# A 128-byte store per partition on the queue of ScalarE, ahead of the bulk stores of a half-rotary kernel

## Chip, cores, metric

One NeuronCore of a Trainium2 chip. The metric is the device time of one execution in microseconds (us), the median of several. The profile's span, from the first to the last instruction, is some 2 us shorter. The medians of the kernel before on different occasions, on chips that the record numbers 1, 2 and 4, differ by up to 0.5 us, so each kernel is compared with runs of the kernel before in the same rounds.

## The reference

```python
batch, seq, heads, dim = (16, 512, 16, 64)          # x: float32; cos, sin: (512, 32)
x1, x2 = x[..., :32], x[..., 32:]
first  = x1[..., :16] * cos[..., :16] - x1[..., 16:] * sin[..., :16]
second = x1[..., :16] * sin[..., :16] + x1[..., 16:] * cos[..., :16]
return np.concatenate([first, second, x2], axis=-1)
```

Half of each head is rotated; the other half, x2, is copied. In a loaded tile x2 is therefore final at once. 33.6 MB come in and 33.6 MB go out.

## The kernel before

The input is cut into four tiles of 8.4 MB, each 128 partitions of 16 sequence rows (64 KB of a partition). Three tiles are held in SBUF at a time. VectorE rotates in place, and each tile is stored from where it was loaded. All bulk transfers go through the queue of SyncE.

```python
ring = const_pool.tile([P, NS, K, H, D], fp32)      # NS = 3 slots, K = 16 rows, H = 16, D = 64
def rows(t, lo, hi):
    return ring[:, t % NS, lo:hi].rearrange("p k h d -> p (k h d)")
def load(t, lo=0, hi=K):
    nc.sync.dma_start(out=rows(t, lo, hi), in_=xf[t, :, lo * R : hi * R])
def store(t, lo=0, hi=K):
    nc.sync.dma_start(out=of[t, :, lo * R : hi * R], in_=rows(t, lo, hi))
# ... zeroed tile, loads of cos and sin on the GpSimd queue ...
load(0, 0, K0)          # K0 = 4:  16 KB per partition
load(0, K0, K)          #          48 KB
load(1)                 #          64 KB
load(2, 0, KC)          # KC = 8:  32 KB
# ... VectorE spreads cos and sin over the partitions ...
rotate(0, 0, K0); rotate(0, K0, 10); rotate(0, 10, K)    # four VectorE instructions each
store(0)
load(2, KC, K)
load(3)                 # same slot as tile 0: waits for store(0)
for t in range(1, T):
    rotate(t, 0, KC); rotate(t, KC, K)
    store(t)
```

A scheduler orders the instructions and puts a semaphore wait wherever two of them touch the same bytes, in SBUF or in the output.

## Time and profile before

| | before |
|---|---|
| device time, median of 4 runs | 162.95 us (162.76 to 162.98) |
| span of the profiled run | 160.9 us |
| VectorE busy | 70% of the span |
| packets of the SyncE queue, share of 16 DMA engines | 97.7% |
| ScalarE | no work |

The profile has three views that matter here. The table of DMA queues says how full the 16 DMA engines are. The chain that ended last says which waits the end hangs on. The timeline says when each transfer was issued. Under these lies the trace's record of every DMA packet: start, duration, size, queue. Put in order, those records make 16 strings, one per engine, in which each packet starts when the one before ends. "Excess" is the duration of a packet above the duration that its size usually has, as a mean over the 16 engines. A "row" is the part of a transfer that lies in one partition; in the records it is one packet. A "turn" is the place in a string where rows of a load are followed by rows of a store, or the reverse; where two queues have work, "one row per turn" means one small row after each packet of the other queue. A transfer has "landed" when its semaphore reports all of it as done. The prediction shows the lines of the page that carry the argument.

### The profile page before, as it was taken

What the parts mean: (1) busy time and instruction counts of PE and PEld (TensorE: products, weight loads), DVE (VectorE), ACT (ScalarE), POOL (GpSimd) and SP (SyncE); (2) the same over time, 40 slices, a digit from 0 to 9 for tenths busy, and PEclk for the clock granted to TensorE, in tenths of its full rate; (3) what the DMA queues carried; (4) which work ended last, traced back from release to release, by engine and by line L of the source; (5) the groups of instructions that cost most, each with busy time, mean ns of one, the idle gap of its engine ahead of it and who ended that gap; (6) DMA issues with size and microseconds to landing.
All of it is one profiled execution on the core that took longest, in us unless ns stands there. A gap on an engine that the chain in (4) does not pass through costs nothing.

```text
span 160.9 us, 116 instructions
## 1 busy us (share of the span) xinstructions
DVE 112.9 (70%) x47; POOL 1.4 (1%) x6
## 2 busy tenths in 40 slices
DVE  1049999999999999999999991699999900000000
POOL 3000000000000000000000000000000000000000
DMA  6999999969999996999996996998998998998992
GB/s 195 554 391 391 391 456 521 521 261 521 391 391 261 521 521 261 521 391 391 472 570 261 521 521 261 521 423 358 521 423 358 521 423 358 521 423 358 521 423 98
DMA packets 1504, 67.24 MB, mean 418 GB/s; under 512 B 192, under 2 KB 192, under 8 KB 224
## 3 DMA queue, kind: packets, MB, share of 16 engines
q1 hardware_dynamic: 1440, 67.11, 97.7%
q0 software_dynamic: 64, 0.13, 0.2%
HBM read 33.69 MB, written 33.55 MB: 418 GB/s over the span
## 4 chain that ended last, share of the span: by engine, by line
DMA 50%; DVE 28%; DVEq 1%; issue 0%; SPq 0%
DMA ring<-in_x_dram 31%; DMA out_dram<-ring 18%; DVE b_t L98 10%; DVE ring L99 10%; DVE ring L100 5%; DVE ring L103 3%; DVEq L142 1%; SPq L55 0%; DVEq L98 0%
## 5 line engine op out<-in xcount | busy, mean ns | idle before, releaser
L98 DVE TENSOR_TENSOR b_t<-ring,table 128x4096 f32<-128x4096 f32 (+2 forms) x9 | 35.6, 3959 | 5.4 <-DMA ring<-in_x_dram 5.2
L99 DVE TENSOR_TENSOR ring<-ring,table 128x4096 f32<-128x4096 f32 (+2 forms) x9 | 35.6, 3950 | 0.3
L100 DVE TENSOR_TENSOR ring<-ring,b_t 128x2048 f32<-128x2048 f32 (+2 forms) x9 | 18.4, 2049 | 0.3
L103 DVE TENSOR_TENSOR ring<-ring,b_t 128x2048 f32<-128x2048 f32 (+2 forms) x9 | 18.4, 2042 | 0.0
L74 DVE LOAD_MASK_SELECT spun<-stage x1 | 0.0, 14 | 8.7 <-DMA stage<-in_sin_dram 8.7
L84 DVE COPY table<-packed 32x1024 f32<-32x1024 f32 x4 | 2.7, 684 | 0.1
L81 DVE COPY packed<-spun 32x512 f32<-32x512 f32 (+3 forms) x4 | 1.7, 416 | 0.1
L61 DVE MEMSET stage<- 128x512 f32 x1 | 0.5, 485 | 0.9 <-PEq L131 0.9
L74 DVE STREAM_SHUFFLE spun<-stage 128x512 f32<-128x512 f32 x1 | 0.7, 722 | 0.0
L63 POOL DMA_DIRECT2D stage<-in_cos_dram x1 | 0.6, 649 | 1.3 <-DVE stage L61 1.3
L64 POOL DMA_DIRECT2D stage<-in_sin_dram x1 | 0.5, 532 | 0.0
L131 POOL MEMSET const-bfloat16-1.0<- 128x1 bf16 x1 | 0.1, 96 | 0.0
L131 POOL MEMSET const-float32-0.0<- 128x1 f32 x1 | 0.1, 93 | 0.2 <-issue 0.2
L131 POOL MEMSET const-float32-1.0<- 128x1 f32 x1 | 0.1, 93 | 0.0
L131 POOL MEMSET const-uint8-127<- 128x1 uint8 x1 | 0.1, 93 | 0.0
## 6 DMA issues: line engine op xcount, KB each, us to landing
ring<-in_x_dram SPq DMA_DIRECT2D x2, 4096.0 KB, 44.9
ring<-in_x_dram SPq DMA_DIRECT2D x1, 6144.0 KB, 21.6
ring<-in_x_dram SPq DMA_DIRECT2D x1, 2048.0 KB, 7.7
stage<-in_cos_dram POOLq DMA_DIRECT2D x1, 64.0 KB, 6.3
stage<-in_sin_dram POOLq DMA_DIRECT2D x1, 64.0 KB, 7.7
out_dram<-ring SPq DMA_DIRECT2D x4, 37.2
ring<-in_x_dram SPq DMA_DIRECT2D x2, 34.7
```

Source lines behind the costliest of these rows:

```text
L61: nc.vector.memset(stage[:, :, :, 0:Q], 0.0)
L63: nc.gpsimd.dma_start(out=spread[:, 0, 0], in_=cosf)
L64: nc.gpsimd.dma_start(out=spread[:, 0, 1], in_=sinf)
L74: nc.vector.stream_shuffle(out=spun[:], in_=stage.rearrange("p t k j -> p (t k) j")[:, :, 0:Q], mask=[j % PQ * REP for j in range(PB)],)
L81: nc.vector.tensor_copy(out=packed[0:n], in_=spun[q * PB : q * PB + n])
L84: nc.vector.tensor_copy(out=table[r * PB : (r + 1) * PB].rearrange("p t k c j -> p (t k) c j"), in_=packed.unsqueeze(2).to_broadcast((PB, ...
L98: nc.vector.tensor_mul(out=b_t, in0=x1, in1=s)
L99: nc.vector.tensor_mul(out=x1, in0=x1, in1=c)
L100: nc.vector.tensor_sub(out=x1[:, :, :, 0:Q], in0=x1[:, :, :, 0:Q], in1=b_t[:, :, :, Q:HF])
L103: nc.vector.tensor_add(out=x1[:, :, :, Q:HF], in0=x1[:, :, :, Q:HF], in1=b_t[:, :, :, 0:Q])
L131: nc = _bacc.Bacc("TRN2", target_bir_lowering=False, num_devices=1)
L142: with _tile.TileContext(nc) as tc:
```

## The change

128 bytes of each partition (columns 32 to 63 of head 0, row 0 of tile 0), already final, go to the output on the queue of ScalarE as soon as the first load has landed. Store 0 writes them again later. The evident intent is to have some writing done, or begun, early on a queue that is otherwise unused.

```diff
     load(0, 0, K0)
+
+    nc.scalar.dma_start(out=of[0, :, HF:D], in_=ring[:, 0, 0, 0, HF:D])
     load(0, K0, K)
     load(1)
     load(2, 0, KC)
```

## The prediction

> **What bounds the kernel now.** I read the page from the top: busy shares first, then the DMA queues, then the chain that ended last, then the timeline of the first 45 us, and last the trace's own record of every DMA packet.
>
> The page, its busy shares, its 40 slices and its DMA queues:
>
> ```profile
> DVE 112.9 (70%) x47; POOL 1.4 (1%) x6
> ...
> DMA  6999999969999996999996996998998998998992
> ...
> DMA packets 1504, 67.24 MB, mean 418 GB/s; under 512 B 192, under 2 KB 192, under 8 KB 224
> ...
> q1 hardware_dynamic: 1440, 67.11, 97.7%
> q0 software_dynamic: 64, 0.13, 0.2%
> ```
>
> VectorE, the only computing engine, works for 70% of the span. The packets of the hardware queue fill 97.7% of all 16 DMA engines' time. The row of digits has no hole after the first slice. 1440 packets are ten transfers of 128 rows plus 16 completion packets each: one packet per partition row, whatever its length, eight rows and one completion per engine and transfer. No ScalarE row exists: that engine does nothing now.
>
> The chain that ended last, in order of time (start, length, what), shows the same from the other side:
>
> ```profile
> 1.17 21.62 DMA ring<-in_x_dram
> ...
> 29.68 1.75 DVE ring L100
> 31.44 1.68 DVE ring L103
> 33.12 0.02 issue
> 33.14 3.38 DVE b_t L98
> ...
> 43.37 29.64 DMA out_dram<-ring
> 73.02 0.02 issue
> 73.03 28.86 DMA ring<-in_x_dram
> ```
>
> The chain runs through VectorE in places, but its DMA pieces are 29 us long for transfers of 8.4 MB, which alone need some 19.3 us: they stand in a queue. So the VectorE pieces are not what sets the end; the queue is full throughout, and the kernel ends when 67.1 MB have passed. The timeline of the start:
>
> ```profile
> 0.74 1.89 SPq L55 DMA_DIRECT2D ring<-in_x_dram  x4
> ...
> 17.87 2.29 DVE L99 TENSOR_TENSOR ring<-ring,table 128x2048 f32<-128x2048 f32 x1
> 20.20 1.22 DVE L100 TENSOR_TENSOR ring<-ring,b_t 128x1024 f32<-128x1024 f32 x1
> 21.34 1.21 DVE L103 TENSOR_TENSOR ring<-ring,b_t 128x1024 f32<-128x1024 f32 x1
> 22.89 3.37 DVE L98 TENSOR_TENSOR b_t<-ring,table 128x3072 f32<-128x3072 f32 x1 [0.34 <-DMA ring<-in_x_dram]
> ...
> 43.37 0.35 SPq L58 DMA_DIRECT2D out_dram<-ring  x1
> ```
>
> Four loads (21.0 MB) are queued by 2.6 us; the first store joins at 43.4 us, about ten before the queue would run dry (the fourth load lands at 53.3 us).
>
> **The packet records.** Ordered by start and put end to end they make 16 strings without holes (0.05 us of idle each, on the mean). A packet has a set duration by size: 159 ns for 4 KB, 608 for 16 KB, 1213 for 32 KB, 1815 for 48 KB, 2418 for 64 KB; a straight line with 12 ns of fixed cost and 36.7 ns per KB, which is 434 GB/s over 16 engines. A string lasts from about 1.9 us to 159.2 us, 157.3 us, and its packets at set durations make 155.4. The difference, 2.3 us by packet durations, lies in three places and almost nowhere else: the first packets (0.65 us, start-up); the last two rows of the load that precedes the first store (0.90 us and 0.47 us above the set duration, mean of 16 engines, starting at 48.7 us); and the last row of the load that precedes the second store (0.25 us). There are only two load-to-store turns, and store-to-load turns show no excess. So the first turn costs 1.37 us and the second 0.25 us. The 1.12 us between them is the price of being the first store, and the one thing that an early small store could buy back.
>
> **What the Trainium skill says.** "DMA: Bandwidth & Descriptors", section "Issuing engines are not separate DMA queues": transfers begun by ScalarE, SyncE or GpSimd run on the same 16 DMA engines and interleave. The trace agrees: the 64 GpSimd packets sit inside the same 16 strings. Section "Queues, rings and completion order" of that page: each engine goes round the queues that have work, a packet at a time. It agrees again: the table loads' 4 KB packets alternate one to one with the 16 KB packets of the load. Section "Specifications" there: under 512 B the engine does read-modify-write. The 128 B rows here are under it; no transfer of data in the present trace is, so its price is open. "Perfetto Trace Analysis", section "What "DMA-bound" means": large descriptors matter where the engines bind. The 12 ns of fixed cost against 2418 ns for 64 KB says this kernel already has them.
>
> **The change part by part.** Nothing is removed; store 0 writes the same bytes again later.
>
> 1. Added on ScalarE: one wait for the first load and one DMA issue. The load lands 7.7 us after 0.74 us, 8.4 us. ScalarE is empty; an issue takes about 0.4 us on SyncE, which issues nothing more at that time. Cost on the path: none.
>
> 2. Added on the DMA engines: 128 rows of 128 B, 16 KB, plus 16 completions; eight rows and one completion per engine. By the straight line (an estimate, below the smallest data packet seen) a row is 12 + 4.6, about 17 ns; a completion is 9 ns in the records: 8 x 17 + 9 = 0.145 us per engine. The engines bind, so all of it is on the path: +0.15 us.
>
> 3. Landing. The first packet of the first load began 1.0 us after its issue, so these packets stand ready at about 9.6 to 10 us. At one small packet per 48 KB packet, nine turns of about 1.83 us bring the landing to about 26 or 27 us; if one turn takes several rows, to about 14 us.
>
> 4. New waits. VectorE writes columns 0 to 31 of each head, the new store reads columns 32 to 63. I expect no wait: in the chain every dependent VectorE pair has an "issue" of 0.02 us between, and L100 and L103, which write interleaved quarters of the same rows, have none, and overlap by 0.08 us. So the tracking sees interleaved columns as separate. Store 0 (same output bytes) and the load of tile 3 into the same slot must wait for the new store; at 43.4 us and 73.0 us both come well after 27 us. Cost: none.
>
> 5. Moved: the first write to the output and the first read of SBUF by these engines, from 48.7 us to about 10 us, on another queue. If the 1.12 us is a price paid once per engine, and a small packet of another queue can pay it while the loads go on, the later turn drops to about 0.25 us: -1.12 us.
>
> Sum if bought back: 162.96 + 0.15 - 1.12 = 161.99 us.
>
> **The rivals.** (a) Price moved, not saved: the excess sits on load packets that were in flight, so whatever stalled there held up other data too, and would do so at 10 us as well; the engines bind at both times. Time: 162.96 + 0.15 = 163.1 us. For it: nothing in the strings ever overlaps. Against it: the stalled packets belonged to the same queue as the store, and another queue may not block it. (b) Small writes cost more than their line: each of eight rows is its own load-to-store turn or a read-modify-write. At 0.25 us a turn, 8 x 0.25 = 2.0 us at most, 162.96 + 2.0 + 0.15 less up to 1.12: 164.0 to 165.1 us. For it: the second turn shows that a turn isn't free. Against it: that turn preceded 64 KB rows, 512 times as long. (c) VectorE waits after all: L99 would start at about 27 instead of 17.9 us, and store 0 be issued at about 52.5 us, with 1.0 us to its first packet: the queue, dry at about 53.2 us, would stand empty some 0.3 us, and over a microsecond if the landing is a turn late. Later stores have slack of several us. Time: 163.3 to 164.5 us. Against it stands the overlap of L100 and L103.
>
> **Range and chances.** I give 0.5 to bought back in whole or part (162.0 to 162.6), 0.35 to moved (163.1), 0.15 to (b) or (c) (163.3 and up). The middle of that is about 162.4 us. The kernel's own spread is 0.2 us. A range of 161.6 to 163.8 us should hold it 8 times in 10. Two per cent is 3.3 us: faster than 159.7 would need more than the whole 2.3 us of excess, so 0.01; slower than 166.2 needs (b) at its full size and more, so 0.02; within 0.97.
>
> **What would show it.** A third queue with 144 packets and 336 instead of 192 packets under 512 B; the first 48 KB and 64 KB packets at their set durations (against a and b); the last two rows before store 0 about 0.12 us instead of 0.69 us above theirs on the mean; VectorE's L99 still at 17.9 us (against c). The prediction is wrong if the 128 B packets take far more than 17 ns, if excess appears on the load packets beside them, or if the 1.37 us stays where it is, which would say that the turn's cost goes with this queue, or these row sizes, and not with being first.

## The result

The changed kernel took 163.16 us (median of 4 runs, 163.06 to 163.28) against 162.95 us. The ratio of the fast runs is 1.0016, 95% interval 0.9999 to 1.0033: the same, if anything 0.2 us slower. The time lies in the predicted range, 0.8 us above the predicted 162.4, and next to the 163.1 of rival (a).

The page of the changed kernel, its DMA queues and the issue that was added (size, then us from issue to landing):

```profile
DMA packets 1648, 67.26 MB, mean 418 GB/s; under 512 B 336, under 2 KB 336, under 8 KB 368
...
q1 hardware_dynamic: 1440, 67.11, 97.5%
q0 software_dynamic: 64, 0.13, 0.2%
q10 hardware_dynamic: 144, 0.02, 0.1%
...
out_dram<-ring ACTq DMA_DIRECT2D x1, 16.0 KB, 19.2
```

The third queue is there with its 144 packets: 128 rows and 16 completions. It takes 0.1% of the engines' time, but its 16 KB need 19.2 us to land. The timeline of the changed kernel:

```profile
8.54 0.37 ACTq L67 DMA_DIRECT2D out_dram<-ring  x1
...
17.67 2.29 DVE L101 TENSOR_TENSOR ring<-ring,table 128x2048 f32<-128x2048 f32 x1
19.99 1.22 DVE L102 TENSOR_TENSOR ring<-ring,b_t 128x1024 f32<-128x1024 f32 x1
21.13 1.21 DVE L105 TENSOR_TENSOR ring<-ring,b_t 128x1024 f32<-128x1024 f32 x1
...
43.43 0.35 SPq L58 DMA_DIRECT2D out_dram<-ring  x1
```

L101 is the former L99, the first VectorE write into the tile that the new store reads. It starts at 17.67 us, ten microseconds before that store lands, so it doesn't wait. Store 0 is issued at 43.43 us, as before (43.37). Store 0 does have the new wait; the waits of SyncE's own queue show it:

```profile
SPq L58 <- DMA out_dram<-ring: 4.8, 1, 4.8
```

SyncE stands at it from 22.9 to 27.7 us, and would have waited for VectorE until 43.4 us anyway. The later pieces of the chain that ended last have the length that they had:

```profile
43.43 29.62 DMA out_dram<-ring
...
73.07 28.91 DMA ring<-in_x_dram
```

What was to shrink did not. The rows around the turn from loads to store 0, from the packet records of both kernels (mean start and end in us, bytes, excess in us):

```
before   47.66 -> 48.87   32768 B   0.002
         48.87 -> 50.99   32768 B   0.903    last two rows of the load
         51.02 -> 52.70   32768 B   0.468
         52.70 -> 55.12   65536 B   0.000    first row of store 0

after    47.66 -> 48.87   32768 B   0.000
         48.87 -> 50.80   32768 B   0.717
         50.81 -> 52.63   32768 B   0.603
         52.63 -> 55.05   65536 B   0.000
```

1.37 us before, 1.32 us after, in the same place. Nor is there any excess where the new rows run: every 48 KB row keeps 1.815 us, every 128 B row is recorded with 13 ns.

### The profile page after: what moved, and what is told of

Its sections match the earlier page's. It is cut to its first block, busy times and chain, and to the rows that moved or that the text cites. A ratio compares the mean times of both kernels' runs of the same rounds, so it can differ in the third digit from the quotient of the medians.

```text
span 161.0 us, 118 instructions
## 1 busy us (share of the span) xinstructions
DVE 112.9 (70%) x47; POOL 1.4 (1%) x6
## 4 chain that ended last, share of the span: by engine, by line
DMA 50%; DVE 28%; DVEq 1%; issue 0%; SPq 0%
DMA ring<-in_x_dram 31%; DMA out_dram<-ring 18%; DVE b_t L100 10%; DVE ring L101 10%; DVE ring L102 5%; DVE ring L105 3%; DVEq L144 1%; SPq L55 0%; DVEq L100 0%
## 5 line engine op out<-in xcount | busy, mean ns | idle before, releaser
L101 DVE TENSOR_TENSOR ring<-ring,table 128x4096 f32<-128x4096 f32 (+2 forms) x9 | 35.6, 3950 | 0.3
## 6 DMA issues: line engine op xcount, KB each, us to landing
out_dram<-ring ACTq DMA_DIRECT2D x1, 16.0 KB, 19.2
```

The lines of the kernel that those rows point to most:

```text
L101: nc.vector.tensor_mul(out=x1, in0=x1, in1=c)
```

## The experiments

Two theories stood at the start. R: the excess belongs to the 32 KB rows that happen to precede store 0, and has nothing to do with being first. F: it belongs to the first store of the SyncE queue, so a store on another queue can't pay it.

**E1, the changed kernel again**, to size its loss.

> The changed kernel as it is, on the chip and in the rounds of the next three, to size its small loss and to see whether its packet pattern repeats. Theory A (the added packets are pure queue time: 8 rows of 13 ns and one completion of 9 ns per engine): +0.11 us, ratio about 1.0007. Theory B (the third queue also costs something at the start or the end): +0.2 us or more, ratio 1.0013 or above. In the packets: the last two 32 KB rows before store 0 are again about 0.7 and 0.6 us above 1.213 us.

162.68 us against 162.59 us, ratio 1.0006 (0.9994 to 1.0019). That agrees with the 0.11 us of queue time of theory A. The excess before store 0 is there again, 1.15 us, though spread as 0.43 and 0.72 us and not as 0.7 and 0.6. Whether the 0.2 us of the first comparison has another part is below what these runs resolve.

**E2, other rows before store 0.**

```diff
-    load(1)
     load(2, 0, KC)
+    load(1)
```

> The kernel before, without the early store, with the loads of tile 1 and of the first half of tile 2 swapped, so that the rows just before store 0 are 64 KB and not 32 KB. Theory R (the 1.37 us of the first load-to-store turn belong to the 32 KB rows): the excess at that turn falls to about 0.25 us, as at the second turn, and the time to about 161.9 us, ratio 0.993. Theory F (it belongs to being the first store of the SyncE queue): the excess stays at about 1.4 us and the time at 163.0 us, ratio 1.000. In both VectorE gets tile 1 later, by some 10 us, and has the slack for it.

162.71 us, ratio 1.0000 (0.9987 to 1.0013). With 64 KB rows the excess is 1.36 us, all on the last row. R has fallen. The timeline of this kernel also clears VectorE:

```profile
43.40 0.35 SPq L58 DMA_DIRECT2D out_dram<-ring  x1
43.79 0.43 SPq L55 DMA_DIRECT2D ring<-in_x_dram  x1
53.31 4.43 DVE L98 TENSOR_TENSOR b_t<-ring,table 128x4096 f32<-128x4096 f32 x1 [9.93 <-DMA ring<-in_x_dram]
```

VectorE is idle for 9.93 us, through the whole turn (48.8 to 52.6 us), so its SBUF traffic isn't what slows those rows.

**E3, 32 KB rows before the second turn.**

```diff
-    load(3)
+    load(3, 0, KC)
+    load(3, KC, K)
```

> The kernel before with the load of tile 3 cut into two halves of 32 KB rows, so that the second load-to-store turn has 32 KB rows as the first has. Theory R (row size): the excess at the second turn rises from 0.25 to about 1.4 us, and the time by about 1.1 us to 164.1 us, ratio 1.007. Theory F (first store of the queue): the second turn stays at about 0.25 us and the time at 163.0 us, ratio 1.000. VectorE can start on half of tile 3 earlier in both; it has slack anyway.

162.53 us, ratio 0.9996 (0.9981 to 1.0010). The second turn has 0.02 us of excess, the first 1.36 us. R falls from this side too.

**E4, the early store on the queue of SyncE itself**, from a zeroed tile, overwritten later by store 0.

```diff
+    nc.vector.memset(zero, 0.0)          # a new 128 x 32 tile
...
     load(0, K0, K)
+    nc.sync.dma_start(out=of[0, :, HF:D], in_=zero)
     load(1)
```

> The kernel before with a 128-byte store per partition (zeros, overwritten later by store 0, so the result is right) on the queue of SyncE itself, behind the two loads of tile 0. Theory F (the price is paid once per queue and engine by its first store): the excess shows on the rows before this small store, at about 22 us, or not at all, and the turn before store 0 falls to about 0.25 us; time between 162.0 us (if the small store hides it) and 163.1 us (if it only moves it). Theory R (row size): the turn before store 0 stays at about 1.4 us and the time is 163.0 to 163.1 us.

162.90 us, ratio 1.0020 (1.0008 to 1.0032). No excess before the small store at 22 us, and 1.14 us before store 0 as ever. F, as stated, has fallen: a first store of the same queue doesn't pay if it is this small. In the records an engine's eight small rows begin some 9 ns apart: from the end of its last 48 KB row to the start of its first 64 KB row there are 84 ns, against 2 ns in the kernel before. So the rows account for 0.08 us of the 0.3 us by which this kernel is longer; the rest is not explained.

**A new theory, F2:** the excess is paid by the first *bulk* store, wherever it stands. Its rivals: G, every turn to a store that has loads behind it costs this much; T, it is tied to store 0 or to its place in time.

**E6, an early bulk store** of zeros, 16 KB per partition, on the queue of SyncE; it adds 2.1 MB.

```diff
     load(0, K0, K)
+    nc.vector.memset(rows(2, KC, KC + K0), 0.0)
+    nc.sync.dma_start(out=of[0, :, 0 : K0 * R], in_=rows(2, KC, KC + K0))
     load(1)
```

> The kernel before with an early bulk store on the queue of SyncE, behind the two loads of tile 0: 16 KB of zeros from each partition, 2.1 MB, into output rows that store 0 overwrites later (the result is right). It adds 8 packets of 0.61 us per engine, 4.9 us of queue time. Theory F2 (the excess is paid by the first bulk store, wherever it stands): an excess of about 1.3 us shows on the last rows before this early store, at about 20 us, and the turn before store 0 falls to 0 to 0.4 us; time about 162.7 + 4.9 = 167.6 us. Theory G (every turn to a large store that is followed by loads costs 1.3 us): both turns show about 1.3 us; time about 168.9 us. Theory T (it is tied to store 0 or to its place in time): nothing at the early store, 1.3 us at store 0; 167.6 us.

167.95 us, ratio 1.0313 (1.0290 to 1.0335), 5.1 us more by the ratio for 4.9 us of added rows. The packet records (columns as above):

```
 18.59 -> 20.42   49152 B   0.017
 20.43 -> 23.52   49152 B   1.276    last row of the load before the early store
 23.52 -> 24.13   16384 B   0.000    first row of the early store
...
 54.96 -> 56.18   32768 B   0.000
 56.17 -> 57.68   32768 B   0.296    last row of the load before store 0
 57.68 -> 60.10   65536 B   0.000    first row of store 0
```

The price has moved to the early store, and store 0 is down to what a second turn costs. G and T fall. But it has *moved*: the total excess is 2.34 us, in the kernel before 2.33.

**E7, a first turn ten microseconds later**, with tile 2 loaded whole before store 0; the trace shows that the scheduler then also put store 1 ahead of load 3.

```diff
-    load(2, 0, KC)
+    load(2)
...
-    load(2, KC, K)
```

> The kernel before with tile 2 loaded whole before store 0, so that the first store comes about 10 us later and is followed by store 1, not by a load. It will be slower for a hole in the queue later; only the turn is looked at. Theory F2 (first bulk store): about 1.3 us of excess on the rows that end at about 62 us. Theory G (a store that is followed by loads): 0 to 0.4 us there. Theory T (place in time): nothing at the turn, some excess at about 49 us.

```profile
43.39 27.23 SPq L58 DMA_DIRECT2D out_dram<-ring  x2
...
82.09 0.34 SPq L55 DMA_DIRECT2D ring<-in_x_dram  x1
```

One run, 171.78 us, its state unknown; only the turn counts. 1.31 us of excess on the last 64 KB row, 58.46 to 62.18 us, nothing at 49 us. The price follows the first bulk store and not the clock, as F2 says.

**E10, how large is bulk?** E6 with 4 KB rows, 0.5 MB.

```diff
+    nc.vector.memset(rows(2, KC, KC + 1), 0.0)
+    nc.sync.dma_start(out=of[0, :, 0:R], in_=rows(2, KC, KC + 1))
```

> The early store of zeros on the queue of SyncE with 4 KB rows in place of 16 KB, 0.5 MB, 1.3 us of queue time: between the 128 B that paid nothing and the 16 KB that paid 1.28 us. If the excess goes with the bytes of store that stand behind loads in flight, a part of it (0.2 to 0.9 us) shows before this store at about 20 us and the rest before store 0; if it is all or nothing above some size, 1.3 us shows at one of the two places and 0 to 0.4 us at the other. Time about 162.7 + 1.3 = 164.0 us in either case.

One run of unknown state, 163.43 us (164.0 expected), against 162.49 us for the kernel before. 1.03 us on the rows before the early store (0.10 and 0.93), 0.00 us before store 0: nearly all of it paid at one place, by rows of 4 KB. The total excess is 1.71 us; E1, with no bulk rows early, happened to have 1.76. Between eight rows of 128 B per engine, which pay nothing, and eight of 4 KB lies the size at which it starts; no run narrows it.

**E5, the new store four times as large**, to test the turns and the wait that hides behind them.

```diff
-    nc.scalar.dma_start(out=of[0, :, HF:D], in_=ring[:, 0, 0, 0, HF:D])
+    # four heads of row 0 in place of one; of4 is of[0] seen as (p, k, h, d)
+    nc.scalar.dma_start(out=of4[:, 0, 0:4, HF:D], in_=ring[:, 0, 0, 0:4, HF:D])
```

> The changed kernel with four times the early store: 128 bytes of four heads, 32 rows of 128 B per engine, on the queue of ScalarE. In the changed kernel each small row waited for one large row of the loads (8 rows and a completion landed 19.2 us after the issue). If that holds, about 22 of the 32 rows are through when the loads end at 53.3 us, the rest follow at once, and store 0, which writes the same bytes and waits for the landing, is issued at about 54 to 55 us and not at 43.4: the DMA engines stand idle for some 2 to 2.5 us, and the time rises by 1.2 to 3 us (ratio 1.007 to 1.018). If several small rows pass in one turn, the landing comes before 43 us, nothing waits, and only 33 packets of 13 ns, 0.4 us, are added (ratio 1.002 to 1.003).

165.28 us, ratio 1.0152 (1.0135 to 1.0170), as expected if one small row passes per turn. The waits of SyncE's queue, and its issue of store 0 in the timeline:

```profile
SPq L58 <- DMA out_dram<-ring: 29.3, 1, 29.3
```

```profile
52.27 0.35 SPq L58 DMA_DIRECT2D out_dram<-ring  x1
```

The wait that took 4.8 us in the changed kernel takes 29.3 us here, and store 0 is issued at 52.27 us, when the loads have ended (51.5 us). The records show 24 of an engine's 32 small rows alternating one to one with packets of the loads from 13.0 us to 51.3 us, and the last eight following within 0.08 us, 9 to 10 ns apart. The DMA engines then stand idle for 1.6 us on the mean. 64 KB of added traffic cost 2.6 us.

E5 has a second message. With no load in flight, store 0's first row shows 0.06 us of excess, as if nothing was to be paid. But the turn from store 0 to the next load, which has no excess elsewhere, shows 0.75 us, and the turn to store 1 shows 0.95 us. So "paid once by the first bulk store" isn't the whole rule: it seems to need bulk stores and loads in flight together. I have not taken that further.

**E8, E8 again, E11: versions without extra bytes.** The finished first quarter of tile 0 goes out on the ScalarE queue; in E11 the second piece as well.

```diff
     rotate(0, 0, K0)
+    nc.scalar.dma_start(out=of[0, :, 0 : K0 * R], in_=rows(0, 0, K0))
     rotate(0, K0, (K0 + K) // 2)
     rotate(0, (K0 + K) // 2, K)
-    store(0)
+    store(0, K0, K)
```

> A version without extra bytes: the quarter of tile 0 that VectorE finishes first (16 KB rows, 2.1 MB) goes out on the queue of ScalarE as soon as it is done, at about 22 us, between the rows of the running loads; store 0 then carries the other three quarters. If the excess is a price of a bulk store's turn out of the loads, it can be paid or hidden there: with alternating rows either eight turns add up (8 times 0.1 to 0.4 us, time 163 to 165 us) or the mixed rows hide the turn, and the total excess falls by about 1 us (161.5 to 162 us). If it is moved only: 162.6 us.

162.50 us against 162.66 us, ratio 0.9984 (0.9965 to 1.0002). The early rows alternate with load rows from 27 us. The excess is spread over them (0.17, 0.07 and smaller), with 0.65 us on the load row before the first two store rows that stand side by side, and there is none before store 0. Total 1.70 us. So the first bulk rows don't pay 1.0 to 1.4 us at one place here: single rows between load rows cost 0.01 to 0.17 us each, and the largest share stands where two of them meet. The sum over these load rows is still 0.97 us (0.98 us when run again), though the stores stand on the other queue.

> The version with the finished quarter of tile 0 on the queue of ScalarE once more, in more rounds, since its first interval (0.9965 to 1.0002) touched 1. Theory H (a part of the excess is really hidden when the first bulk rows go out between load rows): the total excess is again 1.7 us or less against 2.0 to 2.3, ratio 0.997 to 0.999. Theory N (chance): ratio 0.999 to 1.001 and an excess of 2.0 to 2.3 us.

162.44 us against 162.49 us, ratio 0.9992 (0.9974 to 1.0010), total excess 1.78 us. Both ratios are below 1 and neither interval excludes it. The excess lies below the 2.0 to 2.5 us of most other runs, but E1 has 1.76 us and E10 1.71. I don't call it a gain.

> The version with the finished quarter of tile 0 on the queue of ScalarE, and the second piece of it, 24 KB rows, too, at about 33 us; the rest of tile 0 stays with SyncE. Theory H: more of the turn is hidden, excess 1.5 us or less, ratio 0.995 to 0.998. Theory N: as the kernel before, 0.999 to 1.001. Risk: tile 1 comes some 10 us later than before, which VectorE has the slack for.

162.99 us, ratio 1.0036 (1.0002 to 1.0071); slower, if anything. The excess before and during the early stores is 0.92 us on three load rows, and the turn to store 1 at 98 us, 0.02 to 0.41 us in most runs, shows 0.91 us. In this profile, what was saved early came back late.

**E9, all stores on the ScalarE queue.**

```diff
 def store(t, lo=0, hi=K):
-    nc.sync.dma_start(
+    nc.scalar.dma_start(            # and tile 0 stored in three pieces
```

> A version in which all stores go out on the queue of ScalarE, tile 0 in three pieces as each is done, and the loads alone stay with SyncE. Load and store rows then alternate wherever both queues have work. Theory H: the turns go into the alternation and the total excess falls below 1.7 us, time 161.5 to 162.3 us. Against it: while the rows alternate the loads run at half their rate, so tile 1 comes late, VectorE loses its lead and the queues may run dry before the last store: 163 to 168 us.

177.72 us, ratio 1.0931 (1.0901 to 1.0962); the risk came true at more than the named size. The waits of VectorE, the 40 slices, and the store and the load that set the end in the chain of this kernel:

```profile
DVE b_t L98 <- DMA ring<-in_x_dram: 30.8, 3, 26.5
```

```profile
DMA  6998898989699999999897999889999600099885
```

```profile
43.25 38.47 DMA out_dram<-ring
...
81.80 45.61 DMA ring<-in_x_dram
```

While store rows alternate with them, the loads run at less than their full rate, and the other way round. The last piece of store 0 lands 38.47 us after its issue (the whole of store 0 took 29.64 us before), so the load of tile 3 is issued at 81.8 us and not at 73.0, and takes 45.61 us and not 28.86. Tile 3 comes late (VectorE waits 26.5 us for it), store 3 later still, and three slices of the DMA row are empty. The single queue of the kernel before keeps the loads ahead of the stores, and that order is worth 15 us. The total excess rises to 3.15 us; it was expected to fall below 1.7.

The excess of all runs in which it can be set down at one turn, in us per engine, each from one profiled execution. The rows "after" and "E1" are the same kernel, so differences of some 0.2 us are not resolved:

| run | before the early store | before store 0 | before the later store that next follows a load |
|---|---|---|---|
| before | | 1.37 | 0.25 |
| after | 0.00 (128 B rows) | 1.32 | 0.26 |
| E1 | 0.00 (128 B rows) | 1.15 | 0.03 |
| E2 | | 1.36 | 0.11 |
| E3 | | 1.36 | 0.02 |
| E4 | 0.00 (128 B rows, SyncE) | 1.14 | 0.41 |
| E6 | 1.28 (16 KB rows) | 0.30 | 0.12 |
| E7 | | 1.31 | 0.12 |
| E10 | 1.03 (4 KB rows) | 0.00 | 0.06 |

## Why the prediction was right or wrong, point by point

**The bound, and the place of the 2.3 us.** Right. The engines' strings are full in both kernels, and added rows cost about their time where there were enough of them to tell (E6: 5.1 us for 4.9; E10, one run, 0.9 us for 1.3). Two lines of the working don't fit each other: 157.3 less 155.4 is 1.9 us and not 2.3. The durations do add up to 2.3 us of excess; the packets of a string overlap by 3 to 4 ns each, an estimated 0.3 to 0.4 us over the 94 of them, which the prediction left out.

**Steps 1 and 4, the wait and the issue.** Right. VectorE's first write into the tile starts at 17.67 us with the store still in flight. Store 0's new wait ends at 27.7 us, 16 us before it matters; E5 shows what is beyond that slack.

**Step 2, the small rows.** Right in size: 13 ns a row and not 17, 8 x 13 + 9 = 0.11 us for 0.145. E1's 0.09 us between medians can't tell these apart. Where such rows follow each other directly they begin 9 to 10 ns apart (E4, E5), so their records, if anything, say too much. (The 36.7 ns per KB of the straight line are for 1000 bytes; the 64 KB of a row are 65.5 of these.)

**Step 3, the landing.** The total was nearly right, 27.7 us for 26 to 27, but by two errors that cancel. The first row came at 13.1 us and not at 10, 4.6 us after the issue (4.7 us in E5 and E8): two 48 KB rows began in between. Then one row per turn is what happened, but two small rows passed at the end of the load, at 22.2 us, one on either side of its completion packet, so that seven large rows and not nine went by before the last completion.

**Step 5, the first-store price.** This step failed, and with it the half of my chances that lay on 162.0 to 162.6. The excess was real, and it does go with the first store (E6, E7, E10), not with row size (E2, E3). What was wrong is that *any* store would pay it. Rows of 128 B don't, on the ScalarE queue or on SyncE's (E4); rows of 4 KB and 16 KB do. The term of -1.12 us measured -0.05 us, from 1.37 to 1.32 (-0.22 us with E1's profile of the same kernel). The 0.25 us that it took for a later turn was one draw of a quantity that later runs show between 0.00 (E10) and 0.95 us (E5). That the time still lies in the stated range is no evidence for this step: the range held the times of rival (a) and of the price bought back alike. Nor was 162.4 us the middle of the chances given: their median is at the upper edge of the first group, 162.6, and their mean, an estimate with 162.3, 163.1 and 164 us put in, 162.8.

**Rival (a), moved and not saved,** had the right time, 163.1 us, and not the right reason: nothing was moved, the small store paid nothing at all. Its reasoning does hold for the stores that are large enough: in E6 the price comes back in full at the earlier place, and the total excess is 2.34 us against 2.33. The argument against it, that a store on another queue may not block the loads, gets little help from E8: its early rows on ScalarE's queue left 0.97 us of excess on the load rows of SyncE's.

**Rival (b)** doesn't occur: turns for 128 B rows are free in these records. **Rival (c)** doesn't occur at this size.

**Open:** what the engine does in that microsecond; at which row size between 128 B and 4 KB it begins; why the second turn varies from 0.00 to 0.95 us; whether E8's lower excess is a gain; and the 0.2 us of E4 that its small rows don't account for.

## What to carry to other kernels

An early "warming" transfer helps only if it pays the same price as the real one and pays it where the resource is idle; here the small one paid nothing, and the large ones paid in a queue that was just as full. A small transfer beside large rows on another queue is cheap in bandwidth but slow to land, one row per turn, so look at what waits for it before making it any larger. And before spending work on an excess in a trace, size it: here all of it was 2.3 of 163 us.

## What the Trainium skill lacked or had wrong

- "DMA: Bandwidth & Descriptors", section "Queues, rings and completion order", gives a typical packet of 9 to 17 descriptors that is drained before an engine switches queues. The trace doesn't show descriptors. By its records a packet of the SyncE and ScalarE queues is one partition row, from 128 B to 64 KB, and with work on both queues the engines switch after each. So eight 128 B rows per engine were spread from 13.1 to 24.7 us, six of them 1.8 us apart, and 16 KB landed after 19.2 us; with 32 rows the landing took 43.7 us (E5). No page has that landing time, nor the 4.6 us from the issue to the first row beside running loads (1.1 us for the first load, on idle engines).
- No page has the price of the first bulk store among loads: 1.0 to 1.4 us per engine on the load rows just before it, for store rows of 4, 16 and 64 KB and load rows of 32, 48 and 64 KB, and none for store rows of 128 B. It was 0.06 us for a first store with no load in flight (E5), and spread over seven load rows, 0.97 us in sum, where 16 KB store rows alternated with them (E8).
- The same page's section "Specifications" says that an engine does read-modify-write under 512 B. What that costs a store isn't there: these 128 B rows are recorded with 13 ns each, and begin every 9 to 10 ns when nothing stands between them (E4, E5).
